# A transformer block on one core: v's chunk moved behind the attention output's projections, first norm's weights spread by TensorE, four buffers for the gates' sum

## The chip, the cores and the metric

The kernel runs on 1 core of one Trainium2 chip, in one launch. The metric is the device time of the run in microseconds. Three runs of the kernel before took 703.22, 698.96 and 702.06 us (median 702.06).

## The reference

Input are 512 tokens of 1024 float32 values, and the block computes

```
h  = rmsnorm(x) * g1
z  = h @ W_in          # columns: a_q a_k a_v (512 each), a_z 512, beta, alpha,
                       # b_q 512, b_k, b_v, indexer q/k/w, gate_a 1024, gate_b 1024
q,k,v = silu(causal_conv4(a_q | a_k | a_v))            # 8 heads of 64
oA = gated_delta_rule(q, k, v, decay, beta)            # chunks of 64 tokens,
                                                       # a triangular solve in each
oB = sparse_attention(b_q, b_k, b_v, indexer top-k)    # rotary, at most 256 (here 128) keys
x  = x + W_out(sigmoid(gate_a) * P_A(oA) + sigmoid(gate_b) * P_B(oB))
x  = x + two_of_sixteen_experts(rmsnorm(x) * g2)
out = rmsnorm(x) * g
```

## The kernel before, in words

Every large product is made in three passes of a split: a float32 value is written as a high part of reduced width (`whi`, `hTh`, made by ScalarE, L153) and the rest (`wlo`, `hTl`, made by VectorE or GpSimd, L154), and the passes high x high, high x low and low x high are summed in PSUM (`mm3`, L131). The columns of W_in are worked off in chunks, named in the order of the plan (L226 on): kv, iq, bq, qk0, v, qk1, gb0, gb1, pb0, pb1, ga0, z, ga1. A chunk has four quarters; a quarter of a feature chunk is 24 matmuls of 512 columns into one of four accumulator banks (`acc`), and is evacuated at its end: by a tanh for the gates (gb, ga), by a copy for z, and for q, k and v by `conv` (L445): two copies by ScalarE (`xrb`, and `xh` times the last tap), three VectorE operations for the other taps (L452), and a silu (L457). Weights are read and split one quarter ahead into two buffers; the string LOWS names the engine of each low half.

Beside the chunks runs background work, a step or several at each tick. PICKS says how many steps of the selection (`sel`: scores `sn`, searches with MAX and MATCH_REPLACE, L595, L596) a tick does, LOOKS how many of the attention (`att`: exponentials L677, value products into `po`, the rotary embedding of the next query tile on GpSimd, L503 to L506), NORMS how many of the norms of q and k. Three other PSUM banks (`pm`) serve all of this. Where a tick does more steps, they stand earlier in each engine's order; an engine works its own list strictly in that order.

In pb0 and pb1 the systems of the delta rule are set up. Their rows go through DRAM (`lane_n`) into the tile LN, and VectorE solves them in 31 pairs of a product and a sum (`lanes`, L952 and L953, tile X), longest in the middle; the result goes back through DRAM into TT, whose banks are cleared first (`clear_TT`, L962). `sides` transposes q, k and v (L920, L921) and scales them by three VectorE operations for each half tile (L924 to L926, tile rk). In the kernel before, sides and the first ten lane pairs stand in ga0 (the table at L1130: 0, 2, 4, 4), the others in z; then ga1; then the solve, which begins with matmuls of rk and TT. Sides read q, k and v, so those three must be done.

The first norm (L351 to L373): x comes in four tiles of 128 tokens, each is squared and summed by ScalarE (L358), the root is taken on GpSimd (L203), and VectorE multiplies x, the root and the weights g (L362), which a DMA has spread over 128 partitions. TensorE transposes the result. Line L338 on reads the constants. The gates' sum (`ev_a`, L1219) comes behind the projection of the delta rule's output: VectorE adds 1 to the gate and multiplies by the bank (L1221), adds gate b's part (L1222), ScalarE makes the high part (L1224) and GpSimd the low one (L1227).

## Time and profile before

| what | value |
|---|---|
| runs, us | 703.22, 698.96, 702.06 |
| profiled execution, us | 701.66 |
| its span, us | 699.8 |
| mean granted clock of TensorE | 0.98 |
| PE busy | 655.5 us, 94% |
| DVE busy | 526.5 us, 75% |
| ACT busy | 411.6 us, 59% |
| POOL busy | 205.0 us, 29% |

PE is the matrix engine (TensorE) and PEld its weight load, DVE is VectorE, ACT ScalarE, POOL GpSimd, SP the engine that issues DMAs. A busy share is an average over stages with different limits, so the table only says that TensorE has 44 us without work in all; where they lie, and what ends them, is read from the rows further down. PEclk is the clock that TensorE was granted, as a share of its full speed.

### The profile page before, as it was taken

To read this page: it belongs to the slowest core of one execution; us is meant where nothing else is said; L and a number is where in the kernel's file an instruction comes from. 1 tells how busy PE (TensorE), PEld (TensorE's weight loads), DVE (VectorE), ACT (ScalarE), POOL (GpSimd) and SP (SyncE) were. 2 spreads that over 40 slices of the span, in tenths; PEclk is the share of its full clock that TensorE was granted. 3 is DMA by queue.
4 is the path that set the end of the run, shared out by engine and by line. 5 is a ranking of instruction groups with operands and counts; after the bars stand their busy time and mean duration, and the time that the engine had idled before them with its cause. 6 is when DMAs were issued, how large, how long until landed. Compare 5 with 4: busy or idle time off the path is not lost.

```text
span 699.8 us, 10563 instructions
## 1 busy us (share of the span) xinstructions
PE 655.5 (94%) x3460; PEld 538.0 (77%) x3460; DVE 526.5 (75%) x1166; ACT 411.6 (59%) x734; POOL 205.0 (29%) x259
## 2 busy tenths in 40 slices
PE   3999999799899999999999999989999999999992
PEld 2888777567676777778889988878887888888871
DVE  4567799999956466569934666774689999999875
ACT  5345456398968965433333432344258998999863
POOL 2000327516322303231071111660151432333102
PEclk9999999999899999999999999999999999999996
DMA  8333311113021112234355002979779999998963
GB/s 271 118 96 102 91 60 61 60 32 92 29 90 31 61 60 69 76 92 133 92 149 192 2 2 94 380 231 303 256 252 338 333 297 302 300 279 269 282 230 123
DMA packets 84026, 110.77 MB, mean 158 GB/s; under 512 B 17435, under 2 KB 57883, under 8 KB 83840
## 3 DMA queue, kind: packets, MB, share of 16 engines
q1 hardware_dynamic: 79360, 101.70, 44.4%
q0 software_dynamic: 4320, 7.77, 4.5%
q8 instruction: 28, 0.46, 0.3%
q10 hardware_dynamic: 288, 0.59, 0.3%
q14 instruction: 30, 0.25, 0.1%
HBM read 101.22 MB, written 16.78 MB: 169 GB/s over the span
## 4 chain that ended last, share of the span: by engine, by line
PE 70%; DVE 16%; ACT 4%; issue 4%; POOL 3%; DMA 2%; POOLq 0%; ACTq 0%; DVEq 0%
PE acc L129 53%; PE pm L129 7%; DVE xh L452 3%; PE pm L1546 2%; DVE sn L596 2%; DVE ltmp L952 2%; PE po L129 2%; DVE m L595 1%; DVE wlo L154 1%; DVE X L953 1%; POOL wlo L154 1%; POOL mTl L1227 1%; DMA xe<-h2d,ids 1%; PE pg L129 1%; PE ssq L129 1%
## 5 line engine op out<-in xcount | busy, mean ns | idle before, releaser
L153 ACT ACTIVATE whi<-raw 128x1024 fp32r<-128x1024 f32 (+1 forms) x123 | 126.7, 1048 | 99.1 <-PE acc L129 81.2
L154 DVE TENSOR_TENSOR wlo<-raw,whi 128x1024 fp32r<-128x1024 f32 (+1 forms) x100 | 124.1, 1264 | 45.1 <-ACT whi L153 35.3
L154 POOL TENSOR_TENSOR wlo<-raw,whi 128x1024 fp32r<-128x1024 f32 x23 | 57.2, 2489 | 124.6 <-ACT whi L153 116.6
L129 PE MATMUL acc<-whi,xhl 128*128 128x512 f32 x256 | 91.3, 410 | 0.3 <-DVE xhl L1553 0.3
L129 PE MATMUL acc<-hTh,wlo 128*128 128x512 f32 x224 | 89.3, 400 | 1.7 <-POOL wlo L154 1.1
L129 PE MATMUL acc<-hTh,whi 128*128 128x512 f32 x224 | 89.9, 402 | 0.8 <-ACT zb L649 0.8
L129 PE MATMUL acc<-hTl,whi 128*128 128x512 f32 x224 | 89.0, 397 | 0.0
L129 PEld LDWEIGHTS acc<-whi,xhl 128*128 128x128 f32 x256 | 48.1, 188 | 10.2 <-DVE xhl L1553 0.8
L129 PEld LDWEIGHTS acc<-hTh,wlo 128*128 128x128 f32 x224 | 42.6, 190 | 11.6 <-POOL wlo L154 1.7
L129 PEld LDWEIGHTS acc<-hTh,whi 128*128 128x128 f32 x224 | 42.8, 191 | 10.1 <-ACT zb L649 1.0
L129 PE MATMUL acc<-wlo,xhl 128*128 128x512 f32 x128 | 50.4, 394 | 0.0
L129 PEld LDWEIGHTS acc<-hTl,whi 128*128 128x128 f32 x224 | 42.8, 191 | 9.0 <-issue 0.9
L129 PE MATMUL acc<-whi,hTh 128*128 128x456 f32 (+1 forms) x120 | 45.5, 386 | 0.0
L129 PE MATMUL acc<-whi,hTl 128*128 128x456 f32 (+1 forms) x120 | 45.1, 376 | 0.0
L129 PE MATMUL acc<-wlo,hTh 128*128 128x456 f32 (+1 forms) x120 | 44.8, 374 | 0.1
L1591 POOL DMA_INDIRECT accd<-yb,ids x14 | 23.9, 1705 | 58.7 <-ACT ah L153 58.7
L1390 POOL DMA_INDIRECT xe<-h2d,ids x15 | 22.5, 1498 | 42.6 <-PE pm L1546 35.9
L452 DVE SCALAR_TENSOR_TENSOR xh<-xrb,sm,xh 128x511 f32<-128x511 f32 (+2 forms) x36 | 29.8, 879 | 0.0
L129 PE MATMUL acc<-whi,mTh 128*128 128x512 f32 (+1 forms) x72 | 27.9, 388 | 1.8 <-DVE ma L1221 1.8
L595 DVE MAX8 m<-sn 128x8 f32<-128x256 f32 (+2 forms) x48 | 26.6, 557 | 1.1 <-POOL sn L588 0.3
L129 PE MATMUL acc<-whi,mTl 128*128 128x512 f32 (+1 forms) x72 | 27.2, 378 | 0.0
L129 PEld LDWEIGHTS acc<-wlo,xhl 128*128 128x128 f32 x128 | 24.2, 189 | 3.7
(469 smaller groups left out, 1615.6 us busy)
## 6 DMA issues: line engine op xcount, KB each, us to landing
raw<-in_w_in_dram SPq DMA_DIRECT2D x24, 512.0 KB
raw<-in_w_exp_gate_dram SPq DMA_DIRECT2D x42, 256.0 KB
raw<-in_w_exp_up_dram SPq DMA_DIRECT2D x42, 256.0 KB
raw<-in_w_exp_down_dram SPq DMA_DIRECT2D x21, 512.0 KB
raw<-in_w_in_dram SPq DMA_DIRECT2D x16, 256.0 KB
raw<-in_w_out_dram SPq DMA_DIRECT2D x8, 512.0 KB
raw<-in_w_in_dram SPq DMA_DIRECT2D x8, 456.0 KB
x<-in_x_dram SPq DMA_DIRECT2D x4, 512.0 KB
```

The source lines that it names most:

```text
L129: return ins_of(PE.matmul(o, l, r, start=start, stop=stop, skip_group_check=True))
L153: h = ins_of(ACT.activation(hi, src, AF.Copy))
L154: return h, ins_of((lo_eng or DVE).tensor_tensor(lo, src, f32(hi), op=OP.subtract))
L452: DVE.scalar_tensor_tensor(xh[:, j:], xr[:, :512 - j], cw[:, blk, 3 - j:4 - j], xh[:, j:], op0=OP.mult, op1=OP.add)
L595: DVE.max(m8, sn[t])
L596: DVE.match_replace(out=sn[t], in_to_replace=m8, in_values=sn[t], imm_value=-2 * BIG)
L952: DVE.tensor_tensor(tv, skew(flat[0], 0, n, d, 1), skew(flat[1], d, n, d, 32), op=OP.mult)
L953: state["lanes"] = ins_of(DVE.tensor_reduce(skew(flat[0], d, n, 1, 1), tv, axis=AX.X, op=OP.add))
L1227: state["mTl"] = POOL.tensor_tensor(mTl[j][:, i], ma[:, cs], f32(hi[:, cs]), op=OP.subtract)
L1390: return ins_of(POOL.indirect_dma_start(out=xe, out_offset=None, in_=h2d[0:128 * tiles], in_offset=bass.IndirectOffsetOnAxis(ap=idc, axis= ...
L1546: PE.transpose(ps[:, d * 128:(d + 1) * 128], xe[:, k * 128:(k + 1) * 128], C("ident"))
L1591: return ins_of(POOL.indirect_dma_start(out=accd, out_offset=bass.IndirectOffsetOnAxis(ap=idc, axis=0), in_=y, in_offset=None, bounds_chec ...
```

## The change

The diff does three things.

First, the norm's weights come in as one row of 4 KB in place of 512 KB; a row of 128 ones times that row, in two fp32 matmuls with one row of depth, puts them into all partitions of two accumulator banks. The product (now two instructions for each tile, 512 columns each) reads them there. The order constraint on the Squares changes: only the fourth waits, for the first tile's transposed halves.

Second, the order of the chunks becomes kv, iq, bq, qk0, gb0, qk1, gb1, ga0, pb0, pb1, v, z, ga1. The convolution's sums are split from the copies (`conv_sums`): for q and k they follow the fourth copy at once, for v they are dealt out over z, a block of three to each tick. The lanes stand beside v and z (0, 5, 6, 6 and 4, 4, 3, 3 pairs), the sides in the first two quarters of ga1, and the clears and loads of TT behind them. PICKS and LOOKS get other numbers. `xrb` uses other memory.

Third, the gates' sum writes its product back into the PSUM bank and the sum into `ma`, which has four buffers in place of two.

```diff
--- before.py
+++ after.py
@@ -29,8 +29,8 @@
 SELS = (13, 14)
 
 LOWS = "DDDDDDDDDDDDPPDPPPPPPPPPPPPPPPPP"
-PICKS = (1, 5, 5, 4, 4, 4, 4, 2, 2, 4, 4, 4, 2, 3, 4, 4, 3, 0, 0, 0, 0, 0, 0, 0)
-LOOKS = (0, 0, 0, 0, 0, 0, 0, 0, 1, 1, 1, 4, 2, 3, 4, 4, 4, 5, 5, 4, 5, 5, 4, 4)
+PICKS = (1, 5, 5, 4, 4, 4, 4, 2, 2, 4, 4, 4, 4, 4, 4, 4, 0, 0, 0, 0, 0, 0, 0, 0)
+LOOKS = (0, 0, 0, 0, 0, 0, 0, 0, 1, 1, 2, 4, 4, 4, 4, 2, 3, 5, 5, 5, 5, 5, 5, 5)
 NORMS = (0, 0, 0, 0, 0, 0, 0, 0, 0, 1, 1, 1, 1, 1, 1, 0, 0, 2, 1, 1, 1, 1, 2, 2)
 
 A_Q, A_K, A_V, A_Z, A_B = 0, 512, 1024, 1536, 2048
@@ -229,13 +229,13 @@
     want("iq", win, 8, [(I_Q, 512)], *low(LOWS[4:8]))
     want("bq", win, 8, [(1992, 456)], *low(LOWS[8:12]))
     want("qk0", win, 8, [(A_Q, 256), (A_K, 256)], *low(LOWS[12:16]))
-    want("v", win, 8, [(A_V, 512)], *low(LOWS[16:20]))
+    want("gb0", win, 8, [(GATE_B, 512)], *low(LOWS[16:20]))
     want("qk1", win, 8, [(A_Q + 256, 256), (A_K + 256, 256)], *low(LOWS[20:24]))
-    for hf in range(2):
-        want(f"gb{hf}", win, 8, [(GATE_B + 512 * hf, 512)], *low(LOWS[24 + 4 * hf:28 + 4 * hf]))
+    want("gb1", win, 8, [(GATE_B + 512, 512)], *low(LOWS[24:28]))
+    want("ga0", win, 8, [(GATE_A, 512)], *low(LOWS[28:32]))
     for hf in range(2):
         want(f"pb{hf}", w_proj_b[0], 4, [(512 * hf, 512)], DVE)
-    want("ga0", win, 8, [(GATE_A, 512)], DVE)
+    want("v", win, 8, [(A_V, 512)], DVE)
     want("z", win, 8, [(A_Z, 456)], DVE)
     want("ga1", win, 8, [(GATE_A + 512, 512)], DVE)
     for hf in range(2):
@@ -334,7 +334,7 @@
         xts.append(xt)
     g1 = Ft([128, D], F32, "g1", "v0")
     SP.dma_start(xts[0], x[0, 0:128, :])
-    ACT.dma_start(g1, norm1_g[0:1, :].to_broadcast([128, D]))
+    ACT.dma_start(g1[0:1], norm1_g[0:1, :])
     ACT.dma_start(cst[0][:, :128], const[:, :128])
     for t in range(1, T):
         SP.dma_start(xts[t], x[0, t * 128:(t + 1) * 128, :])
@@ -353,13 +353,22 @@
     ss1, rs1, rt1 = (M([128, T], name=n) for n in ("ss1", "rs1", "rt1"))
     turned, rooted, xn = [], [], []
 
+    row1 = M([1, 128], name="row1")
+    DVE.memset(row1, 1.0)
+    g1b = []
+    for i in range(2):
+        g1b.append(acc_tile())
+        mm(g1b[i], row1, g1[0:1, 512 * i:512 * i + 512])
+
     def scaled(t):
-        with after_(turned[t - 2][0] if t > 1 else None):
+        with after_(turned[0][0] if t > 2 else None):
             ACT.activation(junk, xts[t], AF.Square, accum_out=ss1[:, t:t + 1])
         with after_(rooted[-1] if t else None):
             rooted.append(rsqrt_(rs1[:, t:t + 1], ss1[:, t:t + 1], 1.0 / D, rt1[:, t:t + 1]))
         xn.append(Ft([128, D], F32, f"xn{t}", f"tg{t % 2}"))
-        DVE.scalar_tensor_tensor(xn[t], xts[t], rs1[:, t:t + 1], g1, op0=OP.mult, op1=OP.mult)
+        for i in range(2):
+            c = slice(512 * i, 512 * i + 512)
+            DVE.scalar_tensor_tensor(xn[t][:, c], xts[t][:, c], rs1[:, t:t + 1], g1b[i], op0=OP.mult, op1=OP.mult)
 
     scaled(0)
     for t in range(T):
@@ -438,29 +447,39 @@
     vT = [vT2[p // 2][:, p % 2, :] for p in range(4)]
     kq = [Ft([128, T, 2, 128], F32, f"kq{p}", f"kq{p}") for p in range(4)]
 
-    xrb = Ft([128, 4, 512], F32, "xrb", "tg0")
-
-    waiting = []
+    state["xrb"] = Ft([128, 4, 512], F32, "xrb", "tg1")
+
+    waiting, sums = [], []
 
     def conv(blk, fb, acc, dst):
 
-        xr = xrb[:, fb]
+        xr = state["xrb"][:, fb]
         ACT.activation(xr, acc, AF.Copy)
         xh = Ft([128, 512], F32, "xh", "cv", 4)
         out = ins_of(ACT.activation(xh, acc, AF.Copy, scale=cw[:, blk, 3:4]))
-        for j in (1, 2, 3):
-            DVE.scalar_tensor_tensor(xh[:, j:], xr[:, :512 - j], cw[:, blk, 3 - j:4 - j], xh[:, j:], op0=OP.mult, op1=OP.add)
-        waiting.append((dst, xh.rearrange("p (t c) -> p t c", t=T) if len(dst.shape) == 3 else xh))
+        waiting.append((blk, xr, xh, dst))
         if fb == 3:
-            with after_(out):
-                for d, v in waiting:
-                    ACT.activation(d, v, AF.Silu)
+            sums.append(conv_sums(list(waiting), out))
             waiting.clear()
+
+    def conv_sums(blocks, out):
+
+        for n, (blk, xr, xh, dst) in enumerate(blocks):
+            for j in (1, 2, 3):
+                DVE.scalar_tensor_tensor(xh[:, j:], xr[:, :512 - j], cw[:, blk, 3 - j:4 - j], xh[:, j:], op0=OP.mult, op1=OP.add)
+            if n < len(blocks) - 1:
+                yield
+        with after_(out):
+            for blk, xr, xh, dst in blocks:
+                ACT.activation(dst, xh.rearrange("p (t c) -> p t c", t=T) if len(dst.shape) == 3 else xh, AF.Silu)
+        yield
 
     def qk_chunk(g, bg):
         def ev(fb, acc):
             p = 2 * g + fb % 2
             conv(p if fb < 2 else 4 + p, fb, acc, kq[p][:, :, 1 if fb < 2 else 0, :])
+            if fb == 3:
+                drain(sums[-1])
         feat_chunk(f"qk{g}", 8, HT, ev, bg=bg)
 
 
@@ -737,7 +756,7 @@
                 turn(2 + u // 2)
             yield from att_value(*res[u])
 
-    gb = [Ft([128, 4, 512], F32, f"gb{hf}", f"tg{hf}") for hf in range(2)]
+    gb = [Ft([128, 4, 512], F32, "gb0", "tg0")]
 
     def gate_gen(hf):
         def ev(fb, acc):
@@ -773,10 +792,12 @@
     bg = [(behind_projections(), 1)]
     tok_chunk("bq", 8, range(T), HT, ev_w3, bg=bg)
     qk_chunk(0, bg)
-    feat_chunk("v", 8, HT, lambda fb, acc: conv(8 + fb, fb, acc, vT[fb]), bg=bg)
+    for _ in gate_gen(0):
+        tick(bg)
     qk_chunk(1, bg)
     drain(nrm[0])
-    for _ in gate_gen(0):
+    gb.append(Ft([128, 4, 512], F32, "gb1", "tg1"))
+    for _ in gate_gen(1):
         tick(bg)
     drain(sel)
 
@@ -829,7 +850,7 @@
     DVE.tensor_tensor(flat(dl), ps[:, 32:64], flat(nG), op=OP.add)
     ACT.activation(dl, dl, AF.Exp)
 
-    for _ in gate_gen(1):
+    for _ in gate_spill(0):
         tick(bg)
     drain(att, nrm[1])
     for g in range(2):
@@ -1127,13 +1148,13 @@
     rk1 = [Ft([128, 2, 1024], F32, f"rk1{i}", ("obh", "obl")[i]) for i in range(2)]
     place(1, [ke_[1][:, t] for t in range(T)], [rk1[t // 2][:, t % 2] for t in range(T)])
     side, lane = [sides(g) for g in range(2)], lanes()
-    for n, _ in zip((0, 2, 4, 4), gate_spill(0)):
-        tick([(side[0], 1), (side[1], 1), (lane, n)])
-    drain(*side)
-    for t in range(2):
-        clear_TT(t)
-    for n, _ in zip((5, 5, 5, 6), z_chunk()):
+
+    state["xrb"] = rk0[:, 2:4].rearrange("p t (b c) -> p (t b) c", c=512)
+    for n, _ in zip((0, 5, 6, 6), feat_gen("v", 8, HT, lambda fb, acc: conv(8 + fb, fb, acc, vT[fb]))):
         tick([(lane, n)])
+    tick([(sums[-1], 1)])
+    for n, _ in zip((4, 4, 3, 3), z_chunk()):
+        tick([(sums[-1], 1), (lane, n)])
     drain(lane)
 
     angz = GP([128, 64], name="angz")
@@ -1142,8 +1163,15 @@
     for t in range(T):
         zv = zt[t].rearrange("p (h d) -> p h d", h=8)
         POOL.tensor_tensor(zv, zv, angz[:, None, :].to_broadcast([128, 8, 64]), op=OP.mult)
-    lanes_back((0, 1))
-    drain(gate_spill(1))
+    for n, _ in zip((2, 2, 0, 0), gate_spill(1)):
+        if n:
+            tick([(side[0], n), (side[1], n)])
+        else:
+            drain(*side)
+            if not TT:
+                for t in range(2):
+                    clear_TT(t)
+                lanes_back((0, 1))
     feed(state["at"] + 2)
     clear_TT(2)
     lanes_back((2, 3))
@@ -1211,15 +1239,17 @@
     state["RL"] = RL
     state["rawlimit"] = NIN + 1 + NLEFT
     feed_raw(NIN + 1 + NLEFT)
+    EM = Pool("EM")
     state["PW"] = Pool("PW")
     for i in range(2, 4):
         gat.append(ET([128, 2, 512], name=f"gat{i}", tag=("x2T", "h2")[i // 2], bufs=2))
         SP.dma_start(gat[i], gad[i // 2, :, 2 * (i % 2):2 * (i % 2) + 2, :])
 
     def ev_a(i, acc):
-        ma = EA([128, 512], name=f"ma{i}", tag="jk", bufs=2)
-        DVE.scalar_tensor_tensor(ma, gat[i // 2][:, i % 2, :], 1.0, acc, op0=OP.add, op1=OP.mult)
-        DVE.tensor_tensor(ma, ma, gb[i // 4][:, i % 4], op=OP.add)
+        ma = EM([128, 512], name=f"ma{i}", tag="ma", bufs=4)
+
+        DVE.scalar_tensor_tensor(acc, gat[i // 2][:, i % 2, :], 1.0, acc, op0=OP.add, op1=OP.mult)
+        DVE.tensor_tensor(ma, acc, gb[i // 4][:, i % 4], op=OP.add)
         hi = mTh[i // 4][:, i % 4]
         ACT.activation(hi, ma, AF.Copy)
         for j in range(2):
@@ -1260,6 +1290,7 @@
             POOL.memset(b, 0.0)
     F2.close()
     state["PW"].close()
+    EM.close()
 
 
     SL = Pool("SL", side="right")
```

The VectorE list in the lane stage, before (L952 and L953 are the lane rows, L924 to L926 the sides, L154 a weight half of z's chunk):

```order
509 L953 TENSOR_REDUCE X<-ltmp 128x22
510 L952 TENSOR_TENSOR ltmp<-X,LN 128x231
511 L953 TENSOR_REDUCE X<-ltmp 128x21
512 L952 TENSOR_TENSOR ltmp<-X,LN 128x240
513 L953 TENSOR_REDUCE X<-ltmp 128x20
514 L924 TENSOR_TENSOR rk_2530<-pm,eG 128x4x64
515 L925 TENSOR_TENSOR rk_2530<-pm,kds_2483 128x256
516 L926 TENSOR_TENSOR rk_2530<-pm,scv_2484 128x4x64
517 L924 TENSOR_TENSOR rk_2911<-pm,eG 128x4x64
518 L925 TENSOR_TENSOR rk_2911<-pm,kds_2494 128x256
519 L926 TENSOR_TENSOR rk_2911<-pm,scv_2495 128x4x64
520 L154 TENSOR_TENSOR wlo<-raw,whi 128x2x456
```

and as the change has it (L973 and L974 are the lane rows now, L469 the convolution of v, which works in the memory of `rk`):

```order
480 L469 SCALAR_TENSOR_TENSOR xh<-rk_2524,sm,xh 128x511
481 L973 TENSOR_TENSOR ltmp<-X,LN 128x231
482 L469 SCALAR_TENSOR_TENSOR xh<-rk_2524,sm,xh 128x510
483 L974 TENSOR_REDUCE X<-ltmp 128x21
484 L469 SCALAR_TENSOR_TENSOR xh<-rk_2524,sm,xh 128x509
485 L973 TENSOR_TENSOR ltmp<-X,LN 128x240
486 L469 SCALAR_TENSOR_TENSOR xh<-rk_2524,sm,xh 128x511
487 L974 TENSOR_REDUCE X<-ltmp 128x20
488 L154 TENSOR_TENSOR wlo<-raw,whi 128x2x456
489 L973 TENSOR_TENSOR ltmp<-X,LN 128x247
490 L469 SCALAR_TENSOR_TENSOR xh<-rk_2524,sm,xh 128x510
491 L974 TENSOR_REDUCE X<-ltmp 128x19
```

The six side operations are gone from between the lane rows, and an operation of the convolution stands between each two of them, twelve in all.

The TensorE list in ga1, as the change has it (L941 and L942 are the transposes of the sides, the others quarters of ga1):

```order
1236 L941 MATMUL pm<-cst,kq_226 128x128
1237 L942 MATMUL pm<-cst,vT_223 128x128
1238 L941 MATMUL pm<-cst,kq_227 128x128
1239 L942 MATMUL pm<-cst,vT_224 128x128
1240 L941 MATMUL pm<-cst,kq_228 128x128
1241 L942 MATMUL pm<-cst,vT_224 128x128
1242 L129 MATMUL acc<-hTh_118,whi 128x512
1243 L129 MATMUL acc<-hTl_120,whi 128x512
1244 L129 MATMUL acc<-hTh_118,wlo 128x512
1245 L129 MATMUL acc<-hTh_118,whi 128x512
1246 L941 MATMUL pm<-cst,kq_227 128x128
1247 L942 MATMUL pm<-cst,vT_224 128x128
1248 L941 MATMUL pm<-cst,kq_228 128x128
1249 L942 MATMUL pm<-cst,vT_224 128x128
1250 L129 MATMUL acc<-hTl_120,whi 128x512
```

Ahead of these rows stand the 24 matmuls of ga1's first quarter and the first eight transposes. The fourth group of transposes (rows 1246 to 1249) needs a `pm` bank that one of the three groups before it has filled. On VectorE the operations that empty those banks stand behind the lane rows:

```order
539 L973 TENSOR_TENSOR ltmp<-X,LN 128x60
540 L974 TENSOR_REDUCE X<-ltmp 128x2
541 L945 TENSOR_TENSOR rk_2524<-pm,eG 128x4x64
542 L973 TENSOR_TENSOR ltmp<-X,LN 128x31
543 L946 TENSOR_TENSOR rk_2524<-pm,kds_2477 128x256
544 L974 TENSOR_REDUCE X<-ltmp 128x1
545 L1162 COPY angz<-angh 128x64
546 L947 TENSOR_TENSOR rk_2524<-pm,scv_2478 128x4x64
547 L945 TENSOR_TENSOR rk_2524<-pm,eG 128x4x64
548 L946 TENSOR_TENSOR rk_2524<-pm,kds_2477 128x256
549 L947 TENSOR_TENSOR rk_2524<-pm,scv_2478 128x4x64
550 L945 TENSOR_TENSOR rk_2904<-pm,eG 128x4x64
```

The GpSimd list around the memset of the last score tile (L588 before), before:

```order
41 L154 TENSOR_TENSOR wlo<-raw,whi 128x1024 x2
42 L588 MEMSET sn_1137 64x64
43 L154 TENSOR_TENSOR wlo<-raw,whi 128x1024
44 L503 TENSOR_TENSOR ropeA<-bq_812,cos 128x8x32
45 L504 TENSOR_TENSOR ropeB<-bq_812,sin 128x8x32
46 L503 TENSOR_TENSOR ropeA<-bq_812,cos 128x8x32
47 L504 TENSOR_TENSOR ropeB<-bq_812,sin 128x8x32
```

and as the change has it (L607):

```order
41 L154 TENSOR_TENSOR wlo<-raw,whi 128x1024 x2
42 L522 TENSOR_TENSOR ropeA<-bq_821,cos 128x8x32
43 L523 TENSOR_TENSOR ropeB<-bq_821,sin 128x8x32
44 L522 TENSOR_TENSOR ropeA<-bq_821,cos 128x8x32
45 L523 TENSOR_TENSOR ropeB<-bq_821,sin 128x8x32
46 L524 TENSOR_TENSOR bq_821<-ropeA,ropeB 128x8x32
47 L525 TENSOR_TENSOR bq_821<-ropeA,ropeB 128x8x32
48 L607 MEMSET sn_1146 64x64
49 L154 TENSOR_TENSOR wlo<-raw,whi 128x1024 x3
```

The memset stood ahead of a tile's rotary embedding and stands behind the six operations of one now.

## Rows read from the trace of the kernel before

**Rows 1.** The chain that ended last, on the page: share of the span by engine.

```profile
PE 70%; DVE 16%; ACT 4%; issue 4%; POOL 3%; DMA 2%; POOLq 0%; ACTq 0%; DVEq 0%
```

**Rows 2.** DMA view of 0 to 25 us: GB/s in 40 slices, issues with their size.

```profile
GB/s 0 0 20 125 236 380 360 354 311 339 383 402 408 420 415 397 382 363 347 353 310 280 334 320 278 82 0 0 0 0 0 0 0 29 155 376 187 46 197 377
...
g<-in_norm_g_dram ACTq DMA_DIRECT2D x1, 512.0 KB
```

**Rows 3.** Timeline of 0 to 20: start us, us, engine, line, operation, tiles [idle, releaser].

```profile
6.06 1.06 ACT L358 ACTIVATE junk<-x 128x1024 f32<-128x1024 f32 x1 [3.14 <-DMA x<-in_x_dram]
...
8.16 1.28 DVE L362 SCALAR_TENSOR_TENSOR xn<-x,rs,g 128x1024 f32<-128x1024 f32 x1 [8.16 <-POOL rs L203]
...
9.50 3.87 PE L371 MATMUL pm<-cst,xn 128*128 128x128 f32 x16 [9.50 <-DVE xn L362]
...
12.00 1.05 ACT L358 ACTIVATE junk<-x 128x1024 f32<-128x1024 f32 x1
...
17.91 1.94 PE L371 MATMUL pm<-cst,xn 128*128 128x128 f32 x8
```

**Rows 4.** Windows: stretch, length, PE, PEld, DVE, ACT, POOL busy (records), PEclk, DMA, GB/s.

```profile
145.00:160.00 15.00, 13.29 (x61) 9.34 (x60) 14.80 (x36) 14.85 (x34) 5.62 (x6) 1.00 0.12 37
...
185.00:190.00 5.00, 2.53 (x6) 1.64 (x6) 5.00 (x14) 4.98 (x9) 0.89 (x1) 0.72 0.00 0
...
190.00:195.00 5.00, 5.00 (x15) 4.12 (x15) 4.22 (x15) 2.98 (x6) 3.84 (x2) 0.60 0.38 109
...
310.00:350.00 40.00, 39.34 (x192) 33.66 (x191) 37.15 (x83) 13.23 (x18) 3.33 (x6) 1.00 0.36 111
...
350.00:369.00 19.00, 19.00 (x85) 15.62 (x84) 6.62 (x13) 6.08 (x8) 13.67 (x16) 1.00 0.47 136
...
456.00:460.00 4.00, 2.17 (x10) 1.43 (x9) 2.19 (x4) 1.24 (x2) 2.35 (x4) 1.00 0.62 199
...
460.00:464.00 4.00, 4.00 (x11) 3.15 (x12) 1.89 (x3) 2.18 (x3) 1.93 (x4) 0.57 0.10 14
```

**Rows 5.** Waits of PE, 118 to 260: us in total, times, longest.

```profile
PE po L129 <- ACT ph L153: 1.9, 1, 1.9
```

**Rows 6.** Timeline of DVE, 106 to 155: the convolution beside the rope, and without it.

```profile
107.50 11.72 DVE L452 SCALAR_TENSOR_TENSOR xh<-xrb,sm,xh 128x510 f32<-128x510 f32 x10
...
147.69 4.71 DVE L452 SCALAR_TENSOR_TENSOR xh<-xrb,sm,xh 128x510 f32<-128x510 f32 x7
```

**Rows 7.** Timeline of POOL, 108 to 165: rope beside the convolution, memset, rope alone.

```profile
111.78 1.19 POOL L503 TENSOR_TENSOR ropeA<-bq,cos 128x256 f32<-128x256 f32 x1
...
140.32 0.14 POOL L588 MEMSET sn<- 64x64 f32 x1 [0.99 <-DVE sn L586]
...
156.63 0.74 POOL L503 TENSOR_TENSOR ropeA<-bq,cos 128x256 f32<-128x256 f32 x1
```

**Rows 8.** Timeline of DVE, 310 to 354: first lane row, six side operations, end.

```profile
310.79 0.22 DVE L952 TENSOR_TENSOR ltmp<-X,LN 128x31 f32<-128x31 f32 x1 [0.77 <-DMA LN<-lane_n]
...
313.14 0.42 DVE L924 TENSOR_TENSOR rk<-pm,eG 128x256 f32<-128x256 f32 x1 [0.43 <-PE pm L921]
...
315.14 1.21 DVE L154 TENSOR_TENSOR wlo<-raw,whi 128x1024 fp32r<-128x1024 f32 x1
...
353.68 0.18 DVE L1141 COPY angz<-angh 128x64 f32<-128x64 f32 x1
```

**Rows 9.** Tile TT: duration ns min/median/max, first and last start.

```profile
L129 PE MATMUL pm<-rk,TT x64: 270/275/377, 369.1 to 416.4; 128*128 128x128 f32 x64
```

**Rows 10.** Timeline of DVE, 439 to 464: product from a bank, sum alone, sum beside POOL.

```profile
439.94 0.69 DVE L1221 SCALAR_TENSOR_TENSOR ma<-gat,acc 128x512 f32<-128x512 f32 x1 [0.96 <-PE acc L129]
...
444.27 0.69 DVE L1222 TENSOR_TENSOR ma<-ma,gb 128x512 f32<-128x512 f32 x1
...
448.68 2.88 DVE L1222 TENSOR_TENSOR ma<-ma,gb 128x512 f32<-128x512 f32 x1
```

**Rows 11.** Waits of DVE, 440 to 464: us in total, times, longest.

```profile
DVE ma L1221 <- POOL mTl L1227: 5.7, 5, 1.6
```

## The prediction

> **What bounds the kernel now.** I read the page first, and on it the chain that ended last: 70% of it runs over TensorE, 16% over DVE [rows 1]. So a part of the change pays only where it removes one of TensorE's pauses, or the slow stretches behind them, and costs only where it makes one. The table of windows says where these are [rows 4]: each row gives a stretch, its length, the busy time of the engines and the granted clock. Outside the start and the expert stage the pauses that matter here are three: 1.71 us at 145 to 160 (15.00 less 13.29), 2.47 us at 185 to 190, and 1.83 us at 456 to 460. Behind the second, TensorE runs at 0.60 of its clock for 5 us, behind the third at 0.57 for 4 us. Both are stretches in which it fell from the 2.4 GHz level towards the 1.2 GHz level after the pause. Then I read the start as a timeline [rows 3], and the lane stage (310 to 369) row by row, because there DVE is busy for 37 of 40 us [rows 4] and the change gives it other work.
>
> The profiled execution took 701.66 us (span 699.8); the median of the three runs is 702.06, and I make the sum against 701.66. About 1% is what a measurement here can tell from no change: below 695.0 is faster, above 709.1 slower.
>
> **Start: first norm's weights.** Removed is a 512 KB broadcast that is issued just ahead of x's first tile [rows 2]; 4 KB remain. At the 380 GB/s that the transfers reach in that stretch [rows 2] the missing 508 KB are worth 1.37 us, and x's first tile, which the first Square waits for until 6.06 [rows 3], lands so much earlier. Added: a memset, and two fp32 matmuls of 512 columns. Eight times 128 fp32 columns of transposes take 1.94 us [rows 3], so the two cost about 2 us at that rate; they stand ahead of everything on a TensorE that waits until 9.50 anyway, so I cost them at nothing; without that cover they would cost those 2 us. xn (1.28 us [rows 3]) becomes two halves at the 0.69 us of a 512-wide operation that reads PSUM, the price of the gates' product [rows 10]; the transposes of the first half start 0.6 us sooner. That makes 2.0 us. The third Square no longer waits for the first tile's transposed halves (it began at 12.00 [rows 3]), and the fourth waits for those instead of for the second tile's; so the last tile can come sooner by about one more step of that chain, a product of 1.28, 3.3 in all. Bounds: nothing, if the weight tiles queued behind x become the limit, and -3.3. I take **-2.7**, in the middle of 2.0 and 3.3, because the last transposes (17.91 [rows 3]) also wait for DVE, which has the transposed halves to do in between.
>
> **Middle: v's chunk leaves the selection.** Twelve conv operations, eight copies and four silus move from 140 to 155 to the lane stage, and gb0 (four tanh) takes their place; the number of matmuls stays. Ten of the convolution's operations beside the rope on POOL took 11.72 us, seven without it 4.71, or 0.67 each [rows 6, 7]; 12 x 0.67 = 8.0 us leave DVE, which was busy for 14.80 of the 15 us at 145 to 160 [rows 4]. So I take the 1.71 us there as gone. The second pause is po waiting for ph, 1.9 us [rows 5]: ph's copy stood on ACT behind qk1's silus, and those behind DVE's convolution. In the new order 31 accumulating matmuls (7 us) lie between qk1's scores and the next matmul that needs DVE, so 2.47 us of pause and the slow clock go: 5 x 0.40 = 2.0 us at 190 to 195 and 2.53 x 0.28 = 0.7 at 185 to 190 [rows 4]. Together 6.9 us. Against it stands POOL's order: the memset of the last score tile, at 140.32 behind 0.99 us of idle time [rows 7], now stands behind six rope operations of 0.72 us (0.74 less the overlap of one with the next [rows 7]); begun at 139.3, these hold it until 143.7, 3.3 us later. DVE's first search of that tile waits for it, ACT's exponentials stand behind that search and gb0's evacuations behind those, so TensorE runs out of banks. I count the whole 3.3: 6.9 less 3.3 is **-3.6**. Bounds: -6.9 (the banks cover it) and +3.3 (the pauses merely move). The pause at the start of this chunk (about 120) keeps its order and is counted at nothing. Moving gb1 and ga0 one place forward changes only which evacuation ACT does, at nothing, since ACT has room there.
>
> **Lane stage.** In the kernel before DVE's queue runs from 310.79 to 353.68 [rows 8], all lane rows, weight halves and 18 of the side operations among them. Six side operations take from 313.14 to 315.14 [rows 8], 0.333 each. In the new order those 18 (6.0 us) leave, 12 convolution operations (12 x 0.67 = 8.0) come in, one between each two lane rows, and the sides begin only behind the lanes. TensorE does ga1's first quarter, three groups of side transposes and four matmuls more, and then needs a bank that the first side's three operations free: 353.68 - 6.0 + 8.0 + 1.0 = 356.7. After that remain one group of transposes (4 x 0.12, half of the eighth part of 1.94, at the full clock), 20 matmuls, 16 transposes and 48 matmuls; 85 records took 19.00 us at 350 to 369 [rows 4], 0.2235 each. 0.5 + 4.5 + 1.9 + 10.7 = 17.6, so the stage ends at 374.3. The first matmul of TT came at 369.1 [rows 9]: **+5.2**. What is late next is TT itself: its clear and its load move behind the sides, near 367 and 372, and still come before 374. Bounds: nothing (the first rival) and +13 (the third).
>
> **Gates' sum.** DVE's product waits five times, 5.7 us, for POOL to give back one of two buffers [rows 11], and TensorE's banks wait for DVE: 1.83 us of pause and 4 x 0.43 = 1.72 of slow clock, 3.55 together [rows 4]. Four buffers remove the wait. The in-place product keeps each bank for a second operation of 0.69 [rows 10], so I leave 0.6 of it in: **-3.0**; bounds -3.55 and 0, if POOL's rate is what ends the chunk. One sum took 2.88 us beside POOL's weight half against 0.69 alone [rows 10].
>
> The Trainium skill (SBUF — State Buffer, "Who interferes with whom") says that a DVE instruction with two SBUF inputs and a GpSimd instruction that reads SBUF shut each other out. The rows on the convolution [rows 6] and on this sum [rows 10] agree. By it the sum, which now has one input in PSUM, would lose those 2.2 us, which would not change my term, because TensorE did not wait there; and by it the moved convolution would suffer wherever POOL reads, which speaks against this change and is the third rival.
>
> **Sum:** -2.7 - 3.6 + 5.2 - 3.0 = -4.1; 701.66 - 4.1 = **697.6 us**.
>
> **Rivals.**
> 1. *The lane stage costs nothing*: 697.6 - 5.2 = 692.4. For it: DVE was not busy for 2.85 of the 40 us there [rows 4], and TensorE may find the sides' banks free by then. Against it: the order leaves the sides behind all the lane rows. Chance 0.23.
> 2. *The middle returns nothing*: pauses of the same size stand elsewhere, 697.6 + 3.6 = 701.2. For it: the memset behind the rope, and selection steps that are due sooner. Against it: 8 us less on DVE. Chance 0.17.
> 3. *Slower: the convolution meets POOL in the lane stage.* The rope doubled each operation (11.72 / 10 = 1.17 against 0.67 [rows 6]). If POOL's products of keys and decay, which wait for the convolution's buffer there, do the same to all twelve, 12 x 0.50 = 6.0 us join DVE's queue, the pause on TensorE grows by as much, and a stretch as at 190 to 195 follows (2.0): 697.6 + 8.0 = 705.6. It decides as soon as the stage costs more than 9.3 us in place of 5.2 (the other terms give back 9.3). Against it: POOL was busy for 3.33 of 40 us there [rows 4]. Chance 0.11; together with the second (709.2) it passes the 1%, as would a TT that arrives late.
> 4. *The weights' edit doesn't shorten the start*: the weight tiles behind x set TensorE's steady run. 697.6 + 2.7 = 700.3. Chance 0.09.
> The forecast has 0.40.
>
> **Numbers.** The forecast's own range is 693.5 to 700.5. Reaching to most of the first rival and of the second, the range is 689.5 to 703.5, which leaves out the low tail of the first and most of the third. Faster by over 1%: nearly all of the first rival (0.22) and a third of the forecast (0.13), 0.35. Slower by over 1%: 0.08. The rest, 0.57, is within 1%.
>
> **What would show it.** The first Square at about 4.7 and the last transposes near 15; no pause above 1 us between qk1 and gb1, and the clock at 1.00 there; a wait of TensorE for DVE's first side operations, some 17 us before the first TT, and the first TT about 5 us later against the end of pb1 than before; no wait of the product for POOL, and no slow stretch behind it. Wrong is the sum if TensorE does not wait for the sides, or if it waits in gb0 for more than 3 us.

## The result, and the profile after

The changed kernel takes **705.75 us** (median of 20 runs, 701.39 to 709.55) against 701.91 for the kernel before (20 runs, 698.49 to 703.82): ratio 1.0069, interval 1.0052 to 1.0086. It is slower by 0.7%; 697.6 was forecast, with 703.5 as the upper end. (The ratio is not that of the two medians: they differ by 3.8 us, and 0.69% of 702 us is 4.8. Further down, differences between versions in microseconds are differences of such ratios, times 702 us.) The profiled execution is the slowest of its twenty, 709.55 us (span 707.8), 3.8 above its median; where those lie is shown below.

The table gives the length of each stage in microseconds, as differences of first starts that the tile views show: first transposes of keys (`pki`), first product of the systems (`pg`), first lane row, first matmul of TT, first sum of w_out (`xr`), first expert input (`xhl`), last sum of the output. The three columns on the right are versions that the experiments made.

| stage | before | after | norm and gates | memset and low halves | v early |
|---|---|---|---|---|---|
| start, to pki | 43.5 | 42.1 | 40.1 | 40.2 | 42.0 |
| middle, to pg | 222.9 | 224.9 | 222.1 | 221.5 | 221.9 |
| systems, to lanes | 44.4 | 44.2 | 44.2 | 44.3 | 45.0 |
| lane stage, to TT | 58.3 | 65.5 | 58.4 | 65.4 | 58.5 |
| solve and gates' sum, to xr | 108.5 | 104.4 | 104.8 | 104.4 | 104.4 |
| router, to xhl | 46.1 | 46.2 | 46.1 | 46.2 | 46.1 |
| experts | 164.8 | 169.0 | 165.6 | 164.2 | 165.7 |

So the changed kernel won 1.4 at the start and 4.1 in the solve and the gates' sum, and lost 2.0 in the middle, 7.2 in the lane stage and 4.2 in the experts. Without the last, which other runs of the same order don't show, the sum is +3.6, and the medians differ by 3.8. Each column is one execution, and its stretches at a lower clock are its own: the start, the same code in the four columns on the right, takes 40.1 to 42.1. A difference of 1 to 2 us between two columns is therefore shown only where more profiles agree.

The start, as a timeline of after (columns as in [rows 3]):

```profile
3.25 3.75 PE L129 MATMUL acc<-g,row 1*128 1x512 f32 x4 [3.25 <-DMA g<-in_norm_g_dram]
...
4.44 1.06 ACT L365 ACTIVATE junk<-x 128x1024 f32<-128x1024 f32 x1 [1.49 <-DMA x<-in_x_dram]
...
6.54 2.89 DVE L371 SCALAR_TENSOR_TENSOR xn<-x,rs,acc 128x512 f32<-128x512 f32 x4 [5.58 <-POOL rs L203]
...
9.85 1.05 ACT L365 ACTIVATE junk<-x 128x1024 f32<-128x1024 f32 x1
...
15.96 0.60 PE L380 MATMUL pm<-cst,xn 128*128 128x128 f32 x4
```

The first Square begins at 4.44 in place of 6.06, and the last transposes at 15.96 in place of 17.91 [rows 3]. The two matmuls with one row of depth take 3.75 us on an otherwise idle TensorE; VectorE's first product, at 6.54, waited for the root on GpSimd and not for them.

The windows of after (columns as in [rows 4]):

```profile
145.00:150.00 5.00, 2.01 (x8) 1.54 (x8) 4.90 (x19) 3.44 (x9) 0.00 (x0) 0.70 0.00 2
...
150.00:155.00 5.00, 5.00 (x20) 4.29 (x19) 4.54 (x11) 4.50 (x15) 2.37 (x1) 0.62 0.18 42
...
190.00:195.00 5.00, 2.69 (x11) 1.95 (x12) 4.86 (x9) 3.86 (x8) 4.44 (x2) 0.97 0.07 8
...
195.00:200.00 5.00, 5.00 (x24) 4.26 (x23) 2.12 (x12) 3.48 (x9) 2.50 (x6) 0.68 0.63 202
...
350.00:355.00 5.00, 2.18 (x16) 1.66 (x14) 4.72 (x15) 0.80 (x1) 0.00 (x0) 1.00 0.39 107
...
355.00:360.00 5.00, 3.93 (x12) 3.29 (x13) 5.00 (x15) 0.00 (x0) 4.24 (x4) 0.52 0.26 105
...
360.00:365.00 5.00, 5.00 (x25) 4.14 (x24) 1.07 (x3) 1.06 (x1) 3.62 (x6) 0.80 0.28 105
...
452.00:458.00 6.00, 6.00 (x28) 4.81 (x27) 5.87 (x10) 3.92 (x6) 5.55 (x6) 1.00 1.02 401
...
458.00:464.00 6.00, 6.00 (x28) 4.86 (x27) 3.34 (x5) 1.27 (x2) 6.00 (x9) 1.00 0.80 240
...
530.00:535.00 5.00, 2.54 (x13) 2.19 (x12) 2.56 (x4) 1.67 (x3) 1.34 (x2) 0.77 1.05 332
...
535.00:540.00 5.00, 5.00 (x17) 3.96 (x16) 2.97 (x4) 2.97 (x4) 1.02 (x1) 0.55 0.76 254
```

Where the kernel before had pauses at 145 to 160 and 185 to 190 [rows 4], TensorE now stands for 3.0 of the 5 us at 145 and for 2.3 at 190 (with the 1.2 at 185 to 190, 3.5 in two pieces, shown below), and behind each runs at 0.62 and 0.68 of its clock, so most of the time at the lower of its two levels (1.2 of 2.4 GHz). At 350 to 355 there is a new pause, with a clock of 0.52 and 0.80 behind it. At 452 to 464 there is none, where [rows 4] had 1.83 us and a clock of 0.57. At 530 stands the pause of this one execution.

What ended them: waits of PE at 110 to 262 (in total, times, longest),

```profile
PE pm L129 <- DVE mx L689: 3.2, 2, 3.0
...
PE acc L129 <- POOL wlo L154: 1.8, 1, 1.8
...
PE acc L129 <- ACT whi L153: 1.8, 1, 1.8
```

the two waits of 1.8 us, and what ScalarE, VectorE and GpSimd do then,

```profile
190.54 0.50 PE L129 MATMUL acc<-hTh,whi 128*128 128x512 f32 x1 [1.77 <-ACT whi L153]
...
193.73 0.50 PE L129 MATMUL acc<-hTh,wlo 128*128 128x512 f32 x1 [1.77 <-POOL wlo L154]
```

```profile
188.20 1.33 ACT L474 ACTIVATE kq<-xh 128x512 f32<-128x512 f32 x2
189.44 1.99 ACT L153 ACTIVATE whi<-raw 128x1024 fp32r<-128x1024 f32 x2
```

```profile
184.76 6.70 DVE L469 SCALAR_TENSOR_TENSOR xh<-xrb,sm,xh 128x510 f32<-128x510 f32 x10
...
191.85 2.37 DVE L469 SCALAR_TENSOR_TENSOR xh<-xrb,sm,xh 128x509 f32<-128x509 f32 x1
```

```profile
190.56 5.90 POOL L154 TENSOR_TENSOR wlo<-raw,whi 128x1024 fp32r<-128x1024 f32 x2 [7.16 <-ACT whi L153]
```

then VectorE's first search of the last score tile and TensorE's wait behind it, from the timelines of the two engines,

```profile
142.10 0.70 DVE L614 MAX8 m<-sn 128x8 f32<-128x512 f32 x1 [2.73 <-POOL sn L607]
```

```profile
148.01 1.11 PE L129 MATMUL pm<-bkk,bqs 128*128 128x128 f32 x4 [2.99 <-DVE mx L689]
```

the twelve taps of v in the lane stage (min/median/max ns), VectorE's first side operations and TensorE's fourth group of side transposes,

```profile
L469 DVE SCALAR_TENSOR_TENSOR xh<-rk,sm,xh x12: 732/742/969, 321.5 to 336.7; 128x511 f32<-128x511 f32 x4, 128x510 f32<-128x510 f32 x4, 128x509 f32<-128x509 f32 x4
```

```profile
354.53 0.41 DVE L945 TENSOR_TENSOR rk<-pm,eG 128x256 f32<-128x256 f32 x1
...
355.50 0.42 DVE L947 TENSOR_TENSOR rk<-pm,scv 128x256 f32<-128x256 f32 x1
```

```profile
356.07 0.45 PE L941 MATMUL pm<-cst,kq 128*128 128x128 f32 x1 [3.88 <-DVE rk L947]
```

the first matmul of TT (min/median/max ns, first and last start; [rows 9] had 369.1), the waits of VectorE's product in the gates' sum ([rows 11] had 5.7 us for GpSimd), and TensorE's wait for the gather at the experts:

```profile
L129 PE MATMUL pm<-rk,TT x64: 270/275/377, 376.7 to 423.7; 128*128 128x128 f32 x64
```

```profile
DVE acc L1251 <- PE acc L129: 3.3, 3, 1.3
```

```profile
PE pm L1577 <- DMA xe<-h2d,ids: 1.9, 1, 1.9
```

Near 190 the high half `whi` stands on ScalarE behind qk1's silus, which wait for VectorE's taps, and GpSimd makes the low half only then. The search waited 2.73 us for the memset on GpSimd, and TensorE waited 2.99 for a maximum (`mx`) that stands behind the searches in VectorE's order. TensorE asked for a side's bank at 352.2 (356.07 less 3.88) and got it when the third side operation (355.50 and 0.42) was done. The product waits for matmuls now and no longer for a buffer.

In the part on the kernel one sentence is wrong: a quarter of a chunk is a fourth of its depth, and its four banks are evacuated in the last quarter, not in each. No term rests on it.

### The profile page after: what moved, and what is told of

The parts are those of the page before. It is cut to its first block, busy times and chain, and to the rows that moved or that the text cites. A ratio compares the mean times of both kernels' runs of the same rounds, so it can differ in the third digit from the quotient of the medians.

```text
span 707.8 us, 10574 instructions
## 1 busy us (share of the span) xinstructions
PE 663.2 (94%) x3464; PEld 544.4 (77%) x3464; DVE 524.9 (74%) x1171; ACT 411.7 (58%) x734; POOL 205.2 (29%) x259
## 3 DMA queue, kind: packets, MB, share of 16 engines
q1 hardware_dynamic: 79360, 101.70, 44.2%
## 4 chain that ended last, share of the span: by engine, by line
PE 73%; DVE 16%; ACT 4%; issue 3%; DMA 2%; POOL 1%; ACTq 0%; POOLq 0%; DVEq 0%
PE acc L129 56%; PE pm L129 7%; DVE xh L469 3%; DVE sn L615 2%; DVE m L614 2%; PE pm L1577 2%; DVE ltmp L973 2%; DVE wlo L154 1%; PE po L129 1%; DMA xe<-h2d,ids 1%; DVE X L974 1%; ACT whi L153 1%; POOL wlo L154 1%; PE pm L717 1%; PE pg L129 1%
## 5 line engine op out<-in xcount | busy, mean ns | idle before, releaser
L154 DVE TENSOR_TENSOR wlo<-raw,whi 128x1024 fp32r<-128x1024 f32 (+1 forms) x100 | 122.3, 1245 | 49.8 <-ACT whi L153 49.7
L154 POOL TENSOR_TENSOR wlo<-raw,whi 128x1024 fp32r<-128x1024 f32 x23 | 57.5, 2502 | 138.1 <-ACT whi L153 131.8
L129 PE MATMUL acc<-whi,xhl 128*128 128x512 f32 x256 | 92.9, 416 | 0.3 <-DVE xhl L1584 0.3
L129 PE MATMUL acc<-hTl,whi 128*128 128x512 f32 x224 | 90.5, 404 | 0.0
L129 PEld LDWEIGHTS acc<-wlo,hTh 128*128 128x128 f32 x120 | 23.0, 192 | 4.7 <-DVE wlo L154 1.8
```

Of the source, the lines that this page charges most:

```text
L129: return ins_of(PE.matmul(o, l, r, start=start, stop=stop, skip_group_check=True))
L154: return h, ins_of((lo_eng or DVE).tensor_tensor(lo, src, f32(hi), op=OP.subtract))
```

## The experiments

Theory A, read from the two traces: norm and gates' sum pay, and only the moved chunk costs. In every run with the moved chunk the changed tables PICKS and LOOKS came along, so what they do to the middle is not parted from the order of the chunks. The rivals and the later theories (G: GpSimd's low halves stop VectorE) are in the quoted expectations. All ratios are to the kernel before, run on the same chip. "After" without more is the changed kernel; a tap is one of the three VectorE operations of a convolution's block, a low half one `wlo` (L154).

**Norm and gates' sum in the old order.** Edit: the kernel before with the first and the last part of the diff.

> The kernel before with the norm's weights and the gates' sum changed, and the chunks in the old order. By theory A (read from the two traces: the start gave 1.4 us, the gates' sum 3.8, and only the moved chunk cost) it takes 702.0 - 5.2 = about 697, the first matmul of TT comes at about 367.7 and the gates' sum shows no pause of TensorE. By rival B (what the start and the gates' sum give is lost again behind them, at the router and the experts, whose transfers set the end) it takes 700 to 702.

Measured 696.44 us, ratio 0.9946 (0.9926 to 0.9966). That is 3.8 us less, nearer to theory A's 5.2 than to rival B. In its profile the router takes 46.1 as before and the experts 165.6 against 164.8, so little of it, if any, is lost there.

**Gates' sum alone.** Edit: only the hunks of `ev_a` and the pool EM.

> The kernel before with the gates' sum alone changed (product written back into its bank, four buffers). Theory A: the pause of 1.83 us near 457 and the slow clock behind it go, and the time is about 3.8 below the kernel before, 698. If the bank, held for a second operation, takes the place of the buffer, the waits of TensorE for the sum stay at 1 us or more and the gain is under 1.

Measured 699.06 us, 0.9971 (0.9954 to 0.9987). The pause is gone (its stage, from the first matmul of TT to the first sum of w_out, takes 105.0 in place of 108.5); of 3.5 us in the profile the runs keep 2.0, where 3.8 were expected. Where the rest goes is open; in its profile the experts take 168.9 with a clock down to 0.50 at 525 to 530.

**The moved chunk alone.** Edit: after with the old norm and the old gates' sum.

> The changed kernel with the old norm and the old gates' sum: the moved chunk alone, with the tables of steps. Theory A: slower than the kernel before by 2.0 in the middle and 7.2 in the lane stage, about 9, so 711; the pauses are at 145 to 150 (TensorE behind the memset of the last score tile), near 190 and at 352 to 356. Rival C: the moved chunk costs less by itself and the sum of the parts does not add up (for example 705), because the earlier start changes where the pauses fall.

Measured 707.73 us, 1.0095 (1.0072 to 1.0118): 6.7 us slower, between A's 711 and C's 705. The lane stage takes 64.3 (58.3 before) and the middle 223.6 (222.9), so the loss in the lane stage belongs to the moved chunk; of the middle's 2.0 this profile shows only 0.7. With the 3.8 that norm and gates save, the parts make +2.9 against the whole's 4.8; the intervals, some 1.5 us to either side, are too wide to tell the two apart.

**The memset on VectorE.**

```diff
-        POOL.memset(s[0:64, N - 64:N], -BIG)
+        (DVE if t == 3 else POOL).memset(s[0:64, N - 64:N], -BIG)
```

> The changed kernel with one edit: the memset of the last score tile is done by VectorE, so it no longer stands behind the rope on GpSimd. Theory A: VectorE's wait of 2.7 us for it goes, with it TensorE's pause of 3.0 at 145 to 148 and the 1.9 us of slow clock behind it; 3 to 5 us faster than the changed kernel, about 701. Rival D: the selection that now runs earlier only meets the same full VectorE, and the pause moves to the next place (the pauses near 190 grow); less than 1.5 us faster.

Measured 705.56 us, 1.0068 (1.0044 to 1.0093), no change against after (1.0069), and the middle takes 224.8 (224.9). Rival D holds: the pause at 145 falls below 1 us, and this one grows near 188. Timelines of VectorE, GpSimd and TensorE:

```profile
181.85 9.60 DVE L469 SCALAR_TENSOR_TENSOR xh<-xrb,sm,xh 128x509 f32<-128x509 f32 x8
```

```profile
183.28 2.88 POOL L154 TENSOR_TENSOR wlo<-raw,whi 128x1024 fp32r<-128x1024 f32 x1 [4.92 <-ACT whi L153]
...
188.46 2.44 POOL L154 TENSOR_TENSOR wlo<-raw,whi 128x1024 fp32r<-128x1024 f32 x1 [2.29 <-ACT whi L153]
```

```profile
191.98 1.01 PE L129 MATMUL pm<-bkk,bqs 128*128 128x384 f32 x2 [4.32 <-DVE mx L689]
```

Eight tap operations of qk1 take 9.60 us, where the kernel before needs 5.35 for eight; two of GpSimd's low halves lie inside, each a stop of some 2 us for VectorE, and TensorE stands for 4.32 until VectorE has come through. In after the taps begin 5 us later (183.99 against 178.66) and ten of them take 6.70 us; of the twelve a half stops only the last (2.37 us in place of 0.67). That gave theory G.

**The memset and two low halves on VectorE.**

```diff
-LOWS = "DDDDDDDDDDDDPPDPPPPPPPPPPPPPPPPP"
+LOWS = "DDDDDDDDDDDDPPDPPPPPPPPPDDPPPPPP"
```

> The changed kernel with the memset of the last score tile on VectorE as before, and the low halves of gb1's first two quarters made by VectorE in place of GpSimd. In the memset run eight of qk1's convolution operations took 9.60 us beside two of GpSimd's low halves, where the kernel before has 5.35 with GpSimd idle; TensorE waited 4.3 us behind them. Theory G (a low half on GpSimd stops VectorE's two-input operations for its whole 2.4 us, and the new order has put two of them beside qk1's convolution): the eight operations come back to about 5.4 us, VectorE makes the two halves in 1.2 each, TensorE's pause near 188 falls from 4.3 to about 2, and the kernel is 2 to 3 us faster than with the memset alone. Rival H (VectorE is full there whatever GpSimd does): the pause stays at 4 or grows by the 2.4 us of the two halves.

Measured 699.91 us, 0.9994 (0.9974 to 1.0015): 5.2 us faster than with the memset alone, more than the 2 to 3 expected. In the profiles 3.3 of it lie in the middle (221.5 against 224.8) and 1.5 at the start, where the two kernels do not differ. VectorE and GpSimd:

```profile
178.65 6.69 DVE L469 SCALAR_TENSOR_TENSOR xh<-xrb,sm,xh 128x510 f32<-128x510 f32 x10
```

```profile
184.55 3.37 POOL L154 TENSOR_TENSOR wlo<-raw,whi 128x1024 fp32r<-128x1024 f32 x1 [15.94 <-ACT whi L153]
```

Ten taps take 6.69 us, 0.67 each, and GpSimd has nothing to do for 15.94 us before its next half. TensorE's longest wait from 130 to the end of the middle is 1.5. Rival H falls. The Trainium skill (SBUF — State Buffer, "Who interferes with whom") has the rule: a VectorE instruction with two SBUF inputs and a GpSimd instruction that reads SBUF exclude each other. 9.60 against 5.35 for eight taps agrees.

**The two low halves alone.** Edit: only the line above, the memset as in after.

> The changed kernel with only gb1's first two low halves on VectorE, the memset on GpSimd as the change has it. It parts the two edits of the run that was 5 us faster. By theory G the low halves alone give most of it: TensorE's waits near 190 for a weight half (1.8 and 1.8) and the slow clock behind them go, the pause of 3.0 at 145 stays, about 702. If the memset only pays together with them and the low halves alone give nothing, 705 to 706.

Measured 704.22 us, 1.0043 (1.0025 to 1.0061): 1.8 faster than after by the ratios, whose intervals overlap. The middle takes 225.5 in its profile (224.9 in after). The waits of 1.8 for the weight halves are gone, the 2.98 behind the memset stays, and TensorE waits 2.21 us for `mx` at 190 instead. VectorE's last tap and GpSimd:

```profile
189.16 2.43 DVE L469 SCALAR_TENSOR_TENSOR xh<-xrb,sm,xh 128x509 f32<-128x509 f32 x1
```

```profile
188.68 2.38 POOL L154 TENSOR_TENSOR wlo<-raw,whi 128x1024 fp32r<-128x1024 f32 x1 [15.67 <-ACT whi L153]
```

The last tap meets GpSimd's next half and is stopped again. (Part of the 225.5 is a clock down to 0.50 at 120 to 130, ahead of both edits. From GpSimd's low half near 135 to the end of the middle it is 131.7 in after, 131.6 with the memset, 130.9 with the low halves and 128.3 with both.) So neither edit gives more than 1 us in the middle alone, and both give 3.4: with one of the two stops left, VectorE's queue is still late behind it.

**Without v's taps** (left out: the twelve tap operations of v).

```diff
-            for j in (1, 2, 3):
+            for j in (() if blk >= 8 else (1, 2, 3)):
```

> The changed kernel without the twelve tap operations of v's convolution (they are left out, so v is wrong and only the time counts). Theory A (the lane stage is late because the sides stand behind a VectorE queue that the convolution made 8 us longer): the first side operation comes at about 347 in place of 355, TensorE finds its bank when it asks at 352, the pause of 3.9 us and the 3.0 us of slow clock behind it go, the stage from the first lane row to the first matmul of TT falls from 65.5 to about 59, and the kernel is 6 to 7 us faster than the changed one. Rival E (the sides come late by their place in the order, whatever the queue holds): the pause stays above 2 us and the gain is under 3.

Measured 699.40 us, 0.9973 (0.9955 to 0.9992): 6.7 us below after, the lane stage 59.6. TensorE's longest wait at 300 to 385 is now

```profile
PE acc L129 <- DVE wlo L154: 1.3, 1, 1.3
```

and none is for a side; VectorE's first side operation comes at 349.74 (354.53 in after, 347 expected). Theory A holds for the lane stage; E falls.

**Sides one quarter later.**

```diff
-    for n, _ in zip((2, 2, 0, 0), gate_spill(1)):
+    for n, _ in zip((0, 2, 2, -1), gate_spill(1)):
-        if n:
+        if n >= 0:
```

> The changed kernel with the sides one quarter of ga1 later (their transposes in front of the third and the fourth quarter in place of the second and the third). VectorE's work is the same. Theory A: TensorE has 24 more matmuls (5.5 us) to do before it asks for the sides' banks, at 357, when VectorE is through with the lanes (355.3), so the pause goes; TT's clear moves with the sides and becomes the next wait, about 2 us; the stage falls from 65.5 to 60 or 61. Rival F (VectorE's total in the stage is the bound, wherever the sides stand): the stage stays at 64 or more.

Measured 708.55 us, 1.0104 (1.0081 to 1.0127), and the lane stage 65.6, as long as before the edit. That is F's number, not by F's reason: the wait for the sides is gone, and TensorE stands 5.87 us ahead of the first matmul of TT. TensorE, GpSimd and SP:

```profile
377.10 2.05 PE L129 MATMUL pm<-rk,TT 128*128 128x128 f32 x8 [5.87 <-DMA gad<-tga]
```

```profile
369.47 0.96 POOL L983 MEMSET TT<- 128x1024 f32 x1
```

```profile
364.09 2.80 SPq L992 DMA_DIRECT2D TT<-lane_x  x6
...
373.96 2.52 SPq L992 DMA_DIRECT2D TT<-lane_x  x5
```

The second clear of TT comes at 369.47, behind a low half, and the loads behind it until 376.5. (The wait names the spill of the gates, which shares the queue; the loads of TT lie between its pieces.) My step of 2 us for TT was wrong: the clear and the load come behind the sides, and moving the sides moved them to a place where TensorE waits for them. Whether the clear or the shared queue weighs more was not parted.

**All three edits.**

> The changed kernel with three edits: memset on VectorE, gb1's first two low halves on VectorE, and the sides one quarter later. If theories A and G hold, the parts add: 705.6 - 5 (lane stage) - 3 (middle) = about 697 to 698, as fast as the kernel before with the new norm and the new gates' sum (696.4), not faster. If F and H hold, 704 or more.

Measured 704.24 us, 1.0043 (1.0028 to 1.0059). 697 to 698 was expected. The middle keeps its gain (221.5), the lane stage stays at 65.5, and the whole is 3.4 us slower than without the sides' edit: behind TensorE's pause of 5.8 us the solve runs at a clock of 0.94 and takes 50.3 from the first matmul of TT to the last, in place of 47.9 at 1.00. So the sides' edit has to go.

**v early.** v's chunk goes between gb1 and pb0, where VectorE has room; ga0, sides and lanes stand as in the kernel before.

```diff
-    for _ in gate_spill(0):
-        tick(bg)
-    drain(att, nrm[1])
+    feat_chunk("v", 8, HT, lambda fb, acc: conv(8 + fb, fb, acc, vT[fb]), bg=bg)
+    drain(sums[-1], att, nrm[1])
...
+    for n, _ in zip((0, 2, 4, 4), gate_spill(0)):
+        tick([(side[0], 1), (side[1], 1), (lane, n)])
```

> A version from what the runs showed: norm, gates' sum and the order kv, iq, bq, qk0, gb0, qk1, gb1 of the changed kernel, memset and gb1's first two low halves on VectorE; but v's chunk stands between gb1 and pb0, its low halves and its tap operations on VectorE, and ga0, the sides, the lanes, TT's clear and its load stand as in the kernel before. Theory A and G: the middle stays at the 221.5 us (first key transposes to first product of the systems) of the memset-and-low-halves run, the stage from the first lane row to the first matmul of TT falls from 65.4 back to 58.4, no pause of TensorE above 1 us in it; about 693, and below the 696.4 of the norm and gates' sum alone. Rival I: v's taps now meet the last attention units and the systems, and 3 us or more come back between gb1 and the first lane row; 696 or more.

Measured **695.42 us**, 0.9910 (0.9883 to 0.9937), the lowest ratio of all; about 693 was expected. Its interval overlaps that of norm and gates (0.9926 to 0.9966), and no stage of its profile is shorter than there by more than 0.4, so that it beats norm and gates alone is not shown. The lane stage is 58.5, the middle 221.9, the systems 45.0 (0.6 more). VectorE's last taps of v, and TT:

```profile
257.20 5.37 DVE L469 SCALAR_TENSOR_TENSOR xh<-vT,sm,xh 128x509 f32<-128x509 f32 x8
```

```profile
L129 PE MATMUL pm<-rk,TT x64: 270/275/377, 367.4 to 414.4; 128*128 128x128 f32 x64
```

Eight taps in 5.37 us; GpSimd does only two memsets beside them (0.95 and 0.16 us), which read nothing. Of the 3 us of rival I the profile shows 0.6.

**Norm alone.**

> The kernel before with the norm's weights alone changed. By theory A (sum of parts) it takes 1.4 to 3.4 us less than the kernel before, as the difference of the two runs with and without it (696.4 and 699.1) says: about 698.5. If the gain needs the changed gates' sum, it takes 700.5 or more.

Measured 702.69 us, 1.0013 (0.9988 to 1.0038): no gain, against expectation. In its profile the first TT comes at 366.5 in place of 369.1, so the 2.6 us are there at that point. The stage with the old gates' sum then takes 110.7 in place of 108.5, and the router 51.0 in place of 46.1, with hardly a pause. Windows of the router's stretch, of this run and of the norm and gates run:

```profile
477.00:528.00 51.00, 50.10 (x312) 46.05 (x311) 30.79 (x147) 19.97 (x48) 11.43 (x22) 0.90 0.68 229
```

```profile
469.00:516.00 47.00, 46.12 (x315) 41.63 (x313) 31.66 (x148) 20.27 (x48) 11.81 (x22) 1.00 0.73 250
```

TensorE stands for 0.9 us in both, but its clock is 0.90 in the one and 1.00 in the other: 50.10 x 0.10 = 5.0 us. The profiles of the moved chunk alone and of the sides one quarter later have the same 51.0 at 0.90, in other kernels; in these three the clock is at 0.50 for the 5 us that follow the pause, in nine of the other ten the stage is at 1.00. What lets it fall there is not settled, so a gain of the norm at the end of the kernel is not shown by this run.

## Why the prediction was wrong, step by step

By the medians the forecast missed by 7.9 us (3.8 slower where 4.1 faster was forecast). The terms below come to 8.1: 5.6 in the middle, 2.0 in the lane stage, 1.3 at the start, less 0.8 in the gates' sum.

- **Start, -2.7.** Measured -1.4 in the profile of after, where a stretch at 15 to 20 lost 1.1 us to a clock of 0.72 (3.97 x 0.28), and -3.4 in that of norm and gates, where the clock stayed at 1.00. The ten profiles with the new norm have 40.1 to 42.1 for this stage, the three with the old one 43.5 to 45.1. The mechanism is right; the two matmuls took 3.75 us where 2 were priced, under the cover that was named.
- **Middle, -3.6: the step that failed.** Measured +2.0. The new pause behind the memset came as worked out (2.73 on VectorE and 2.99 on TensorE against 3.3; it reached TensorE by the `pm` bank that `mx` reads, not by gb0's evacuations), though the slow clock behind it, 1.9 us (5 x 0.38 at 150 to 155), was not in the sum. The step that is wrong is "31 accumulating matmuls (7 us) lie between qk1's scores and the next matmul that needs DVE, so 2.47 us of pause and the slow clock go". Matmuls that accumulate need their weight halves, and these need ACT and GpSimd: they waited 1.8 us for `whi`, queued behind qk1's silus, and 1.8 for the `wlo` that GpSimd made from it. The silus were late because VectorE's queue was: with the stop of 2.7 us at the memset taken away, the taps begin 5 us earlier. And GpSimd's halves, which in the kernel before came after qk1's taps, met VectorE: in after at a small operation just ahead of the taps (2.29 us at 181, 0.18 in the low-halves run) and at the last tap (2.37), in the memset run at eight taps (9.60 in place of 5.35). I had named that exclusion, and looked for it only at v's taps in the lane stage. The six profiles with the new order and one stop or both left have 223.6 to 225.6 for the middle, the four with the old order 221.6 to 222.9, the two with both stops mended 221.5. So mended the new order saves 0.1 to 1.4 us there: the 1.71 and 2.47 us that I took as gone go only in small part even then.
- **Lane stage, +5.2.** Measured +7.2. The place, the wait and its cause are as forecast (bank at 355.9, 356.7 in the sum); the size lacks the slow clock behind the pause, 2.9 us (3.93 x 0.48 and 5.00 x 0.20), so the rest of the sum was 0.9 too dear. I priced that only in the third rival. (The products 3.93 x 0.48 and 5.00 x 0.20 are estimates of what the clock cost, busy time times the missing share.)
- **Gates' sum, -3.0.** In the profile -3.8 (60.3 to 56.5 from the last matmul of TT to the first sum of w_out), as the mechanism said; the runs of it alone show -2.0. The sum, which reads one input from PSUM now, takes 0.67 to 0.69 us in all eight cases (2.88 in one before [rows 10]), though GpSimd is busy for 11.55 of the 12 us at 452 to 464.
- **Experts, nothing.** +4.2 in the profiled execution, by a wait of 1.9 us for a gather and a clock of 0.55 behind it. The seven profiles of its variants in the experiments (moved chunk alone, memset, halves, both, taps, sides, all three) show 163.5 to 166.3 for that stage, so this is that execution's and not the change's. (Of all profiles, the ten with the new gates' sum have 163.5 to 169.0 there and the three with the old one 163.7 to 164.8; a small loss that comes with the new sum is not excluded.)
- **The rivals.** The second (701.2) was the nearest: the middle returned nothing, and lost. The third had its mechanism, but not where it put it: v's taps took 0.73 to 0.97 us each in the lane stage, not 1.17, and the stop came at qk1's. The upper end left out that the second and a dearer lane stage could hold together.

## What to carry to other kernels

Price a new pause of TensorE with the slow stretch behind it: here the pauses of 3.0 and 3.9 us cost an estimated 1.9 and 2.9 more. Look at several profiles before a stage is said to have won or lost 2 us. When the order changes, list for every run of two-input VectorE operations what GpSimd now does beside it, not only for those that moved. And move work to where its engine has room (gb1 to pb0 here), not to where the chain to the next stage already runs over that engine.
